# Another division of an output projection between attention's end and the loop of norm and router

## The chip, the cores and the metric

One core of a Trainium2 chip runs the whole block. The metric is device time in microseconds (us), the median of several executions. The engines are PE (TensorE, matrix products), DVE (VectorE), ACT (ScalarE), POOL (GpSimd) and SP (SyncE, which here only issues transfers). Each works through its own instructions in the order in which they stand; they wait for each other by semaphores.

## The reference

One bidirectional encoder layer on 1024 tokens of width 1024, in float32. The part around the change is this:

```python
a_out = diff_attention(q, k, v, lam, subln_g[l], lambda_init)      # 4 heads of 128 channels
p_out = multiscale_pool(u, w_pool[l], pool_scale[l])               # the mixer: 4 groups of 128
mix = jnp.concatenate([a_out, p_out], axis=-1) @ w_out[l]
x = x + g1[:, None] * mix
h = rms_norm(x, norm2_g[l]) * (1.0 + sc2[:, None]) + sh2[:, None]
y = hierarchical_moe(h, w_router_group[l], b_router_group[l], w_router_expert[l],
                     b_router_expert[l], w_gate[l], w_up[l], w_down[l])
x = x + g2[:, None] * y
```

The router picks for each token the best of 4 groups and the best two of the 8 experts in it. Each of the 32 experts then works on its tokens: `silu(x @ w_gate) * (x @ w_up) @ w_down`.

## The kernel before, in words

Tokens are worked on in 8 tiles `t` of 128 rows. A float32 product is made of three fast ones (`mm3`): each operand is split into a high and a low part, and high x high, high x low and low x high are added in PSUM.

The output projection adds up 8 blocks of 128 channels: blocks 0 to 3 are the attention heads, blocks 4 to 7 the mixer. `PARTS = [[4, 5, 6, 7], [0], [1], [2], [3]]` names five parts of it: part 0 is the mixer (4 blocks, 24 products of 128x512 for a tile), parts 1 to 4 are heads 0 to 3 (6 products each). `out_part(t, i)` makes part `i` of tile `t` on PE into a PSUM tile `pm` and adds it to the residual tile `X2[t]` on DVE: the mixer by a plain addition, a head by a scaled one, since each head has a factor by row (`Y8`) from its own norm. The pool of the `pm` tiles has two buffers.

The stages in question, in the order of the program:

- **The fill.** `attend(n)` is one step of a software pipeline through the 32 pairs of head and row tile. Its last steps, `n` from 33 to 40, have little left to do. `FILL` names them, and behind each stands the mixer part of one tile. What the projection reads is loaded by `loads`, one or two transfers behind each step (`LOADS`), in the order of that list.
- **Heads 0 and 1.** Parts 1 and 2 of all tiles follow in two rounds (`SECOND = 3`), with two loads of expert weights (`w_next`) behind each tile of the second (`EARLY1`).
- **The loop of norm and router**, `t` from 0 to 8. Round `t` makes parts 3 and 4 of tile `t`. It transposes tile `t - 1` (`flip`, PE into PSUM tiles `ph`, copied by ACT to `h2T`). It stores `X2[t]` and takes the sum of its squares (`norm2`). Then it finishes the norm of tile `t - 1` (`norm2_out`: DVE scales, POOL adds the shift `shB`, POOL's queue stores `xnd`; the last tile's shift is added by DVE) and makes its router logits (`router`, PE into `plg`).
- **Routing in batches** of tiles (`BATCH`): `route(c)` is cut into three pieces, all on DVE but for two exponentials on ACT. `rank(c)` counts on PE (`pR`) and DVE (`pk`), `place(c)` writes the tokens into the experts' lists by products on PE (`lists`). `PLAN` says behind which round each piece stands: `r` a piece of `route`, `k` `rank`, `p` `place`, `w` idle products that keep PE at work.
- **The expert loop.** POOL gathers the first tiles by the lists; then per expert 72 products of 128x512 and 12 transposes, over 12 weight tiles of 512 KB that ACT and DVE split into high and low.

SBUF has 50 slabs of 128x1024 float32. SP's loads wait in their queue until the slab that they are to fill has been read for the last time. `EARLY` says how many loads of expert weights are issued behind each round of the loop.

Where a row of the profile says L82, the helper at line 82 issued the instruction; tiles tell them apart.

Of the kernel before, what the change touches and what calls it, by code (L numbers as in the profile page):

```python
# [14 lines left out]
OP = mybir.AluOpType  # L15
# [6 lines left out]
T = S // P  # L22
KD = D // P
NH = 4
# [17 lines left out]
LOADS = {n: 1 for n in range(20, 30)}  # L42
FILL = range(33, 41)
LOAD_RATE = 2
SECOND = 3
EARLY1 = {(2, t): 2 for t in range(8)}
BATCH = [0, 0, 1, 1, 1, 2, 2, 2]
PLAN = {2: "r0", 3: "r0 r0", 4: "k0", 5: "p0 r1 r1", 6: "r1", 7: "k1", 8: "p1 w10 r2 r2 r2 k2 w4 p2"}
EARLY = {**{t: 2 for t in range(8)}, 8: 8}
ROWS = [5, 8, 11, 13]  # L50
MODS = {0: 1, 1: 2, 2: 2, **{m: 3 for m in range(3, 12)}}
WO = 7
# [16 lines left out]
def block_kernel(ctx: ExitStack, tc: tile.TileContext, A):  # L69
# [134 lines left out]
    def w_next():  # L204
        g = len(RW)
        if g < len(seq):
            e, i = seq[g]
            RW[e, i] = slab(f"we{e}_{i}")
            dma(RW[e, i], A["w_exp"][e, i])

    with tc.tile_pool(name="ps0", bufs=2, space=PSUM) as psum, tc.tile_pool(name="ps1", bufs=2, space=PSUM) as psum1, \
# [570 lines left out]
            X2[t] = slab(f"x{t}")  # L782
            dma(X2[t], A["x"][t])

        loads = [(mixer_load, 0, i, x) for i in range(2) for x in range(2)]
        loads += [(wo_load, k, x) for k in PARTS[0] for x in range(2)] + [(x_load, t) for t in range(4)]
        loads += [(mixer_load, 1, i, x) for i in range(2) for x in range(2)] + [(x_load, t) for t in range(4, T)]
        loads += [(wo_load, k, x) for k in range(NH) for x in range(2)]

        def out_part(t, i, hs=(0, 1)):  # L790

# [12 lines left out]
                dve.scalar_tensor_tensor(x, p, Y8[:, i - 1, t:t + 1], x, op0=OP.mult, op1=OP.add)  # L804

        n = FIRST
        early = [(t, 0) for t in range(T)]
        while n < N + 9 or later:
            attend(n)
            for _ in range(LOADS.get(n, LOAD_RATE if n > max(LOADS) else 0)):  # L810
                if loads:
                    fn, *args = loads.pop(0)
                    fn(*args)
            if n in FILL:
                out_part(*early.pop(0))
            n += 1
        while loads:
            fn, *args = loads.pop(0)
            fn(*args)
        for t, i in early:  # L820
            out_part(t, i)
        for i in range(1, SECOND):
            for t in range(T):
                out_part(t, i)
                for _ in range(EARLY1.get((i, t), 0)):
                    w_next()

        RK = cst.tile([P, T, 2], F32, name="RK")
        cums = cst.tile([P, T + 1, NE], BF16, name="cums")
# [25 lines left out]
        def norm2_out(t):  # L855

            xn = XN.pop(t)
            dve.scalar_tensor_tensor(xn, X2[t], RS[:, t:t + 1], MB[0], op0=OP.mult, op1=OP.mult)
            (dve if t == T - 1 else pool).tensor_tensor(xn, xn, MB[1], op=OP.add)
            (act_dma if t == T - 1 else pool_dma)(xnd[t * P:(t + 1) * P], xn)  # L860

        RT, LG = {}, {}
# [121 lines left out]
        steps = {}  # L984
        for t in range(T + 1):
            if t < T:
                for i in range(SECOND, 4):
                    out_part(t, i)
            if t >= 1:
                flip(t - 1, 0)  # L990
                flip(t - 1, 1)
            if t < T - 1:
                out_part(t, 4)
                norm2(t)
            elif t == T - 1:
                out_part(t, 4, (0,))
                out_part(t, 4, (1,))
                norm2(t)
            if t >= 1:
                norm2_out(t - 1)  # L1000
                router(t - 1)
            for _ in range(EARLY.get(t, 0)):
                w_next()
            for x in PLAN.get(t, "").split():
                c = int(x[1:])
                if x[0] == "r":
                    if c not in steps:
                        steps[c] = route(c)
                    next(steps[c], 1)
                elif x[0] == "k":  # L1010
                    rank(c)
                elif x[0] == "w":
                    warm2(c)
                else:
                    place(c)
# [321 lines left out]
```

## Time and profile before

| | us |
|---|---|
| Median of 3 runs | 1204.95 |
| The runs | 1195.96, 1205.28, 1204.95 |
| The profiled execution | 1198.64 |
| Its span, first to last instruction | 1196.9 |

| Engine | busy us | share of the span |
|---|---|---|
| PE | 1105.3 | 92% |
| DVE | 1014.7 | 85% |
| ACT | 732.4 | 61% |
| POOL | 396.8 | 33% |

The span divides into attention and what stands ahead of it (to 412.8 us), the stages that the change touches (412.8 to 572.3), the expert loop (to about 1140) and the final norm. Busy shares over the whole span say little here, since the stages have different limits; the rows below are read stage by stage. "Granted clock" (PEclk) is the share of TensorE's full clock.

### The profile page before, as it was taken

The numbers are of one execution on the slowest core, as the hardware profiler recorded it, in microseconds if no ns is written. First come the engines' busy times: TensorE is split into PE (matmuls) and PEld (weight loads), VectorE is DVE, ScalarE is ACT, GpSimd is POOL, SyncE is SP. The second block draws the span as 40 slices with busy tenths as digits, with TensorE's granted clock in tenths as the row PEclk, the third lists the DMA queues.
The fourth block names the chain that finished last, engine by engine and source line by source line (L and its number), as shares of the span: only waits on it lengthen the run. The fifth ranks groups of instructions, "written<-read, shape, count | busy, mean of one in ns | idle before, by whom it ended". The sixth has DMA issues, their size and how long they took to land.

```text
span 1196.9 us, 15760 instructions
## 1 busy us (share of the span) xinstructions
PE 1105.3 (92%) x5319; PEld 903.4 (75%) x5319; DVE 1014.7 (85%) x1187; ACT 732.4 (61%) x937; POOL 396.8 (33%) x260
## 2 busy tenths in 40 slices
PE   6696989899999999988999999999999999999975
PEld 6485866677888887777788888888888888888742
DVE  5969898868999725899899999999999999999927
ACT  5443222248888600222788888888888888888812
POOL 3546977737888600343111011011111111101001
PEclk8698999899999999977999999999999999999988
DMA  9836499489563784566699999999999999999155
GB/s 369 314 116 241 125 397 323 174 296 278 136 188 108 299 312 161 164 243 245 197 363 380 383 380 391 392 388 387 384 386 384 388 382 384 384 387 380 46 211 220
DMA packets 102950, 349.60 MB, mean 292 GB/s; under 512 B 15986, under 2 KB 16914, under 8 KB 102866
## 3 DMA queue, kind: packets, MB, share of 16 engines
q1 hardware_dynamic: 91266, 323.08, 73.9%
q0 software_dynamic: 11456, 24.96, 5.6%
q8 instruction: 43, 0.70, 0.2%
q10 hardware_dynamic: 144, 0.52, 0.1%
q14 instruction: 41, 0.34, 0.1%
HBM read 309.95 MB, written 55.33 MB: 305 GB/s over the span
## 4 chain that ended last, share of the span: by engine, by line
issue 46%; PE 26%; DVE 16%; POOL 6%; DMA 4%; ACT 1%; SPq 0%; POOLq 0%; DVEq 0%; ACTq 0%
PE pm L82 7%; PE s L82 4%; DVE wt L82 4%; PE po L82 4%; POOL x L82 4%; PE pz_v L82 3%; POOL yd L82 2%; PE pz_u L82 2%; PE pw L82 2%; DVE rt L82 2%; DMA wt<-in_w_ada 2%; DVE fy L82 1%; PE yp L82 1%; DVE wil L82 1%; DVE xn L82 1%
## 5 line engine op out<-in xcount | busy, mean ns | idle before, releaser
L82 DVE TENSOR_TENSOR wl<-we,wh 128x1024 fp32r<-128x1024 f32 x384 | 458.4, 1222 | 39.6 <-ACT wh L82 34.4
L82 ACT ACTIVATE wh<-we 128x1024 fp32r<-128x1024 f32 x384 | 399.7, 1058 | 60.5 <-PE pg L82 29.0
L82 PE MATMUL pg<-wh,xs 128*128 128x512 f32 x1024 | 338.8, 397 | 0.0
L82 PEld LDWEIGHTS pg<-wh,xs 128*128 128x128 f32 x1024 | 192.8, 188 | 39.1 <-ACT xs L82 0.2
L82 PE MATMUL pg<-wl,xs 128*128 128x512 f32 x512 | 200.0, 391 | 0.0
L82 POOL DMA_INDIRECT yd<-y,ix x32 | 32.1, 1004 | 479.6 <-ACT y L82 466.9
L82 PE MATMUL py<-wh,hth 128*128 128x512 f32 x512 | 171.9, 397 | 1.0 <-ACT hth L82 0.7
L82 PEld LDWEIGHTS py<-wh,hth 128*128 128x128 f32 x512 | 96.1, 188 | 21.8 <-DVE hth L82 1.2
L82 PEld LDWEIGHTS pg<-wl,xs 128*128 128x128 f32 x512 | 96.7, 189 | 18.2
L82 PE MATMUL py<-wl,hth 128*128 128x512 f32 x256 | 99.9, 390 | 0.0
L82 ACT ACTIVATE e<-s,mx 128x1024 f32<-128x1024 f32 x64 | 71.6, 1119 | 42.6 <-DVE mx L82 40.3
L82 DVE SCALAR_TENSOR_TENSOR wt<-wt,cB 128x1024 f32<-128x1024 f32 x48 | 91.1, 1943 | 0.8 <-ACT cB L82 0.8
L82 PE MATMUL s<-k,sq 128*128 128x512 f32 x256 | 74.0, 412 | 10.4 <-ACT e L82 10.3
L82 DVE TENSOR_REDUCE mx<-s 128x1 f32<-128x1024 f32 x64 | 78.2, 1221 | 6.0 <-PE s L82 3.2
L82 POOL TENSOR_TENSOR e<-e,e 128x1024 f32<-128x1024 f32 x32 | 76.5, 2390 | 2.7
L82 PE MATMUL po<-wh,v 128*128 128x256 f32 x256 | 60.7, 301 | 0.0
L82 PEld LDWEIGHTS s<-k,sq 128*128 128x128 f32 x256 | 44.8, 193 | 19.6 <-ACT e L82 13.1
L82 POOL DMA_INDIRECT x<-xnd,ix x32 | 46.2, 1442 | 35.3 <-PE px L82 13.6
L82 PEld LDWEIGHTS py<-wl,hth 128*128 128x128 f32 x256 | 48.2, 188 | 9.4
L82 ACT ACTIVATE xn<-x 128x1024 f32<-128x1024 f32 x7 | 7.4, 1062 | 74.1 <-DVE x L82 68.8
L82 POOL TENSOR_SCALAR e<-e,cc 128x1024 f32<-128x1024 f32 x32 | 39.2, 1225 | 37.2 <-DVE cc L82 16.7
L82 DVE SCALAR_TENSOR_TENSOR x<-pm,Y,x 128x1024 f32<-128x1024 f32 (+1 forms) x33 | 41.2, 1249 | 7.8 <-PE pm L82 6.0
(227 smaller groups left out, 2035.8 us busy)
## 6 DMA issues: line engine op xcount, KB each, us to landing
we<-in_w_exp SPq DMA_DIRECT2D x384, 512.0 KB, 6.9
wt<-in_w_ada SPq DMA_DIRECT2D x48, 512.0 KB, 8.7
win<-in_w_in SPq DMA_DIRECT2D x16, 512.0 KB, 9.1
k<-kd SPq DMA_DIRECT2D x32, 256.0 KB, 9.4
woB<-wod SPq DMA_DIRECT2D x16, 512.0 KB, 6.0
fy<-yd SPq DMA_DIRECT2D x16, 512.0 KB, 10.1
xt<-in_xT SPq DMA_DIRECT2D x8, 512.0 KB, 7.7
wo<-in_w_out SPq DMA_DIRECT2D x8, 512.0 KB, 6.6
```

Of the source, the lines that this page charges most:

```text
L82: ins = getattr(self.eng, op)(*args, **kw)
```

## The change

The mixer part and heads 0 to 2 change places. In the fill, each step is now followed by heads 0, 1 and 2 of one tile (parts 1 to 3). The two rounds of heads 0 and 1 behind the fill are gone. Round `t` of the loop makes the mixer part of tile `t`, then, behind the transposes of tile `t - 1`, head 3 as before. `loads` follows: first the residual tiles and the weights of heads 0 to 2, last the mixer tiles. DVE adds the shift for all tiles. The batches of routing are 3, 3 and 2 tiles instead of 2, 3 and 3, and `PLAN` places their pieces up to a round later. The loads of expert weights ahead of the expert loop are 32 instead of 40, none ahead of round 4.

```diff
--- before.py
+++ after.py
@@ -42,11 +42,9 @@
 LOADS = {n: 1 for n in range(20, 30)}
 FILL = range(33, 41)
 LOAD_RATE = 2
-SECOND = 3
-EARLY1 = {(2, t): 2 for t in range(8)}
-BATCH = [0, 0, 1, 1, 1, 2, 2, 2]
-PLAN = {2: "r0", 3: "r0 r0", 4: "k0", 5: "p0 r1 r1", 6: "r1", 7: "k1", 8: "p1 w10 r2 r2 r2 k2 w4 p2"}
-EARLY = {**{t: 2 for t in range(8)}, 8: 8}
+BATCH = [0, 0, 0, 1, 1, 1, 2, 2]
+PLAN = {3: "r0", 4: "r0 r0", 5: "k0", 6: "p0 r1 r1", 7: "r1 k1", 8: "p1 w10 r2 r2 r2 k2 w4 p2"}
+EARLY = {4: 6, 5: 2, 6: 4, 7: 4, 8: 16}
 ROWS = [5, 8, 11, 13]
 MODS = {0: 1, 1: 2, 2: 2, **{m: 3 for m in range(3, 12)}}
 WO = 7
@@ -782,10 +780,10 @@
             X2[t] = slab(f"x{t}")
             dma(X2[t], A["x"][t])
 
-        loads = [(mixer_load, 0, i, x) for i in range(2) for x in range(2)]
-        loads += [(wo_load, k, x) for k in PARTS[0] for x in range(2)] + [(x_load, t) for t in range(4)]
-        loads += [(mixer_load, 1, i, x) for i in range(2) for x in range(2)] + [(x_load, t) for t in range(4, T)]
-        loads += [(wo_load, k, x) for k in range(NH) for x in range(2)]
+        loads = [(x_load, 0), (x_load, 1)] + [(wo_load, k, x) for k in range(3) for x in range(2)]
+        loads += [(x_load, t) for t in range(2, T)] + [(wo_load, 3, x) for x in range(2)]
+        loads += [(wo_load, k, x) for k in PARTS[0] for x in range(2)]
+        loads += [(mixer_load, a, i, x) for a in range(2) for i in range(2) for x in range(2)]
 
         def out_part(t, i, hs=(0, 1)):
 
@@ -804,7 +802,7 @@
                 dve.scalar_tensor_tensor(x, p, Y8[:, i - 1, t:t + 1], x, op0=OP.mult, op1=OP.add)
 
         n = FIRST
-        early = [(t, 0) for t in range(T)]
+        early = list(range(T))
         while n < N + 9 or later:
             attend(n)
             for _ in range(LOADS.get(n, LOAD_RATE if n > max(LOADS) else 0)):
@@ -812,18 +810,14 @@
                     fn, *args = loads.pop(0)
                     fn(*args)
             if n in FILL:
-                out_part(*early.pop(0))
+                t = early.pop(0)
+                for i in range(1, 4):
+                    out_part(t, i)
             n += 1
         while loads:
             fn, *args = loads.pop(0)
             fn(*args)
-        for t, i in early:
-            out_part(t, i)
-        for i in range(1, SECOND):
-            for t in range(T):
-                out_part(t, i)
-                for _ in range(EARLY1.get((i, t), 0)):
-                    w_next()
+        assert not early
 
         RK = cst.tile([P, T, 2], F32, name="RK")
         cums = cst.tile([P, T + 1, NE], BF16, name="cums")
@@ -856,7 +850,7 @@
 
             xn = XN.pop(t)
             dve.scalar_tensor_tensor(xn, X2[t], RS[:, t:t + 1], MB[0], op0=OP.mult, op1=OP.mult)
-            (dve if t == T - 1 else pool).tensor_tensor(xn, xn, MB[1], op=OP.add)
+            dve.tensor_tensor(xn, xn, MB[1], op=OP.add)
             (act_dma if t == T - 1 else pool_dma)(xnd[t * P:(t + 1) * P], xn)
 
         RT, LG = {}, {}
@@ -984,8 +978,7 @@
         steps = {}
         for t in range(T + 1):
             if t < T:
-                for i in range(SECOND, 4):
-                    out_part(t, i)
+                out_part(t, 0)
             if t >= 1:
                 flip(t - 1, 0)
                 flip(t - 1, 1)
```

Three places show what that does to the order. First DVE, at the first step of the fill. `wl` and `mxl` are attention's last low parts, `x` is a residual tile and `pm` a part of the projection (its number is the part). Before:

```order
L82 SCALAR_TENSOR_TENSOR mxl_2_2984<-po_3434,mxh_2_2983 128x256
L82 TENSOR_TENSOR x_3477<-pm_0_3562,x_3477 128x1024
L82 TENSOR_TENSOR wl_1_3527<-pw_6_1_3545,wh_1_3525 128x4x128
L82 TENSOR_TENSOR wl_0_3526<-pw_7_0_3588,wh_0_3524 128x4x128
L82 COPY ss_3516<-po_3434 128x2
L82 TENSOR_TENSOR x_3479<-pm_0_3621,x_3479 128x1024
```

Now:

```order
L80 SCALAR_TENSOR_TENSOR mxl_2_2984<-po_3434,mxh_2_2983 128x256
L80 SCALAR_TENSOR_TENSOR x_2833<-pm_1_3562,Y_251,x_2833 128x1024
L80 SCALAR_TENSOR_TENSOR x_2833<-pm_2_3570,Y_251,x_2833 128x1024
L80 SCALAR_TENSOR_TENSOR x_2833<-pm_3_3578,Y_251,x_2833 128x1024
L80 TENSOR_TENSOR wl_1_3527<-pw_6_1_3545,wh_1_3525 128x4x128
L80 TENSOR_TENSOR wl_0_3526<-pw_7_0_3586,wh_0_3524 128x4x128
L80 COPY ss_3516<-po_3434 128x2
L80 SCALAR_TENSOR_TENSOR x_2891<-pm_1_3619,Y_251,x_2891 128x1024
```

One plain addition becomes three scaled ones, and attention's next instructions stand behind three evictions instead of one.

Second PE, in the loop: `ph` are the transposes of a tile, `plg` its router product, `woB` weights of the projection, `mxh` and `mxl` the heads' high and low parts, `mu` the mixer's. Before, from one router product to the head behind the next transposes:

```order
L82 MATMUL plg<-wr,h2T_4081 128x36 x8
L82 MATMUL pm_3_4126<-woB_0_3814,mxh_2_2983 128x512
L82 MATMUL pm_3_4126<-woB_1_3816,mxh_2_2983 128x512
L82 MATMUL pm_3_4126<-woB_0_3814,mxl_2_2984 128x512
L82 MATMUL pm_3_4126<-woB_0_3814,mxh_2_2983 128x512
L82 MATMUL pm_3_4126<-woB_1_3816,mxh_2_2983 128x512
L82 MATMUL pm_3_4126<-woB_0_3814,mxl_2_2984 128x512
L82 MATMUL ph_0_4135<-ident,x_3479 128x128 x4
L82 MATMUL ph_1_4141<-ident,x_3479 128x128 x4
L82 MATMUL pm_4_4147<-woB_0_3846,mxh_2_2983 128x512
L82 MATMUL pm_4_4147<-woB_1_3848,mxh_2_2983 128x512
L82 MATMUL pm_4_4147<-woB_0_3846,mxl_2_2984 128x512
```

Now, the last two of the mixer part's 24 products up to the next router product:

```order
L80 MATMUL pm_0_4044<-woB_1_3705,mu_3774 128x512
L80 MATMUL pm_0_4044<-woB_0_3703,mu_3776 128x512
L80 MATMUL ph_0_4071<-ident,x_3296 128x128 x4
L80 MATMUL ph_1_4077<-ident,x_3296 128x128 x4
L80 MATMUL pm_4_4083<-woB_0_3520,mxh_2_2983 128x512
L80 MATMUL pm_4_4083<-woB_1_3522,mxh_2_2983 128x512
L80 MATMUL pm_4_4083<-woB_0_3520,mxl_2_2984 128x512
L80 MATMUL pm_4_4083<-woB_0_3520,mxh_2_2983 128x512
L80 MATMUL pm_4_4083<-woB_1_3522,mxh_2_2983 128x512
L80 MATMUL pm_4_4083<-woB_0_3520,mxl_2_2984 128x512
L80 MATMUL plg<-wr,h2T_4070 128x36 x8
```

Head 2 (`pm_3`) has made room for the mixer part (`pm_0`) between a router product and the next transposes.

Third DVE, from the last eviction of tile 7 on. `xn` is the normed tile, `gB` its scale, `rt` a batch of routing, `ob`, `cums` and `mv` its last piece, `pk` its ranking. Before:

```order
L82 SCALAR_TENSOR_TENSOR x_3711<-pm_4_4502,Y_251,x_3711 128x512
L82 SCALAR_TENSOR_TENSOR xn_4507,ss<-x_3711 128x1024
L82 TENSOR_SCALAR n2r_m<-ss 128x1
L82 SCALAR_TENSOR_TENSOR xn_4440<-x_3709,RS,gB 128x1024
L82 SCALAR_TENSOR_TENSOR rt_4458<-plg,RS,rbias 128x36
L82 TENSOR_TENSOR pk_4530<-pR_4531,rt_4236 128x6x32
L82 TENSOR_REDUCE RK<-pk_4530 128x6
L82 TENSOR_TENSOR pk_4530<-slots,RK 128x256 x3
L82 SCALAR_TENSOR_TENSOR xn_4507<-x_3711,RS,gB 128x1024
L82 TENSOR_TENSOR xn_4507<-xn_4507,shB 128x1024
```

Now, from the norm of tile 6 on:

```order
L80 SCALAR_TENSOR_TENSOR xn_4356<-x_3477,RS,gB 128x1024
L80 TENSOR_TENSOR xn_4356<-xn_4356,shB 128x1024
L80 SCALAR_TENSOR_TENSOR rt_4482<-plg,RS,rbias 128x36
L80 TENSOR_TENSOR rt_4186<-rt_4186 128x3x32 x2
L80 TENSOR_TENSOR ob<-rt_4186 128x96
L80 TENSOR_TENSOR cums<-cums,ob 128x32 x3
L80 COPY rt_4186<-tok_104 128x6x2
L80 TENSOR_TENSOR rt_4186<-rt_4186 128x3 x2
L80 TENSOR_TENSOR mv<-rt_4186 128x576
L80 TENSOR_TENSOR pk_4504<-pR_4505,rt_4186 128x6x32
L80 TENSOR_REDUCE RK<-pk_4504 128x6
L80 TENSOR_TENSOR pk_4504<-slots,RK 128x256 x3
```

The addition of the shift and the last piece of routing (from `rt` 128x3x32 to `mv`) now stand between the norm of tile 6 and the ranking, and so ahead of the norm of tile 7.

## Rows read from the trace of the kernel before

**Rows 1.** Busy time by stretch: us, busy us (x instructions) by engine, PEclk, DMA share, GB/s

```profile
412.80:464.10 51.30, 50.44 (x251) 42.55 (x249) 12.50 (x23) 2.69 (x7) 2.44 (x2) 1.00 0.66 248
464.10:489.80 25.70, 25.70 (x103) 17.73 (x101) 21.74 (x18) 0.00 (x0) 0.00 (x0) 1.00 0.54 196
489.80:548.70 58.90, 48.87 (x276) 42.02 (x276) 53.10 (x104) 16.29 (x32) 27.94 (x35) 0.87 0.65 224
548.70:572.30 23.60, 18.97 (x117) 17.67 (x114) 20.42 (x59) 6.23 (x9) 7.37 (x6) 0.72 0.68 247
600.00:1100.00 500.00, 500.00 (x2367) 413.53 (x2365) 466.09 (x451) 428.83 (x480) 71.19 (x57) 1.00 1.00 384
```

**Rows 2.** Waits of SP's DMA queue, 560 to 1150 us: waited for, us, times, longest

```profile
SPq L103 <- DVE wl L82: 414.4, 353, 21.5
```

**Rows 3.** Timeline of PE at the end of the fill: start us, us, what

```profile
447.63 16.63 PE L82 MATMUL pm<-woB,mu 128*128 128x512 f32 x72
464.10 0.62 PE L82 MATMUL pm<-woB,mxh 128*128 128x512 f32 x2
```

**Rows 4.** Timeline of DVE, heads 0 and 1 (idle before and its releaser in brackets)

```profile
479.43 2.68 DVE L82 SCALAR_TENSOR_TENSOR x<-pm,Y,x 128x1024 f32<-128x1024 f32 x2 [0.37 <-PE pm L82]
```

**Rows 5.** Timeline of PE, one round of the loop

```profile
495.24 1.87 PE L82 MATMUL plg<-wr,h2T 128*128 128x36 f32 x16
496.94 0.70 PE L82 MATMUL pm<-woB,mxh 128*128 128x512 f32 x2
...
498.41 1.04 PE L82 MATMUL ph<-ident,x 128*128 128x128 f32 x8
499.20 0.71 PE L82 MATMUL pm<-woB,mxh 128*128 128x512 f32 x2
...
500.67 1.87 PE L82 MATMUL plg<-wr,h2T 128*128 128x36 f32 x16
```

**Rows 6.** Timeline of PE, placing, router products, first expert product

```profile
525.27 1.11 PE L82 MATMUL lists<-mv,pk 128*128 128x96 f32 x8
...
533.93 3.63 PE L82 MATMUL plg<-wr,h2T 128*128 128x36 f32 x16 [3.81 <-ACT h2T L82]
...
551.17 3.47 PE L82 MATMUL plg<-wr,h2T 128*128 128x36 f32 x16
...
572.30 0.79 PE L82 MATMUL pg<-wh,xs 128*128 128x512 f32 x1
```

**Rows 7.** Timeline of DVE, end of the loop and tail

```profile
539.48 0.42 DVE L82 TENSOR_TENSOR rt<-rt 128x96 f32<-128x96 f32 x2
...
543.93 2.13 DVE L82 SCALAR_TENSOR_TENSOR x<-pm,Y,x 128x1024 f32<-128x1024 f32 x2
546.27 0.75 DVE L82 SCALAR_TENSOR_TENSOR x<-pm,Y,x 128x512 f32<-128x512 f32 x1 [0.21 <-PE pm L82]
...
554.71 1.23 DVE L82 TENSOR_TENSOR xn<-xn,shB 128x1024 f32<-128x1024 f32 x1
```

**Rows 8.** Timeline of POOL, one add of the shift

```profile
540.40 2.35 POOL L82 TENSOR_TENSOR xn<-xn,shB 128x1024 f32<-128x1024 f32 x1
```

**Rows 9.** Timeline of DVE, instructions beside an add on POOL and the same later

```profile
540.23 2.76 DVE L82 TENSOR_TENSOR cums<-cums,ob 128x32 bf16<-128x32 bf16 x3
...
550.63 2.84 DVE L82 TENSOR_TENSOR pk<-slots,RK 128x256 f32<-128x256 f32 x3
...
561.32 0.59 DVE L82 TENSOR_TENSOR cums<-cums,ob 128x32 bf16<-128x32 bf16 x3
...
563.62 1.09 DVE L82 TENSOR_TENSOR pk<-slots,RK 128x256 f32<-128x256 f32 x3
```

**Rows 10.** Weight loads on SP, to 575 us and after: ns min/median/max, first and last start

```profile
L103 SPq DMA_DIRECT2D we<-in_w_exp x40: 327/333/1364, 421.1 to 550.2; - x40
...
L103 SPq DMA_DIRECT2D we<-in_w_exp x344: 327/328/357, 579.9 to 1092.1; - x172
```

**Rows 11.** Busy time by stretch, behind one gap of PE

```profile
533.00:541.00 8.00, 7.07 (x31) 6.38 (x32) 7.44 (x24) 2.56 (x6) 1.93 (x4) 0.57 0.67 244
```

## The prediction

> **What bounds the kernel now.** I read the table by stage first [rows 1]. From 600 to 1100 us, in the expert loop, PE is busy all of the time at full clock; DVE has 466 of 500 us, and the transfers run at 384 GB/s. Is PE or the transfer the limit there? The DMA queue of SP answers: it stood 414 us waiting for DVE to finish with a weight buffer, 353 times [rows 2]. A queue that waits for free buffers is not the one that is late, so the expert loop goes at PE's pace and its length is fixed. What can move is its first product, at 572.30, where the tail ends [rows 1].
>
> Ahead of it lie four stretches [rows 1]: the fill (412.8 to 464.1), heads 0 and 1 (to 489.8), the loop of norm and router (to 548.7), and the tail. The reader is to see who idles in each. In the fill PE has 50.4 of 51.3 us and DVE only 12.5. In the next, both are nearly full, alternating. In the loop DVE has 53.1 of 58.9, PE 48.9 and the clock is 0.87: DVE ends the waits. So DVE idles early and is late afterwards. The change trades work between those two places.
>
> **The change, step by step.** No matrix product is added or dropped. Times are the trace's.
>
> *Fill.* The 72 products between the two starts in [rows 3] take (464.10 - 447.63) / 72 = 0.229 us each, so a mixer part of 24 takes 5.49. Eight are 43.9, which leaves 51.3 - 43.9 = 7.4 us for the end of attention. Afterwards there are 24 parts of six products. At PE's pace one takes 1.37; but with two buffers of PSUM, PE and DVE alternate as they do now for heads 0 and 1: 2.68 + 0.37 = 3.05 us per two parts [rows 4]. I take that: 24 x 1.525 = 36.6, plus 7.4, is 44.0. Bounds: 40.3 if PE sets the pace (24 x 1.37 + 7.4); 48 if an eviction of about 1.3 more stands in front of three of attention's last DVE steps. The stretch of heads 0 and 1, 25.7 us, disappears. The fill ends at 412.8 + 44.0 = 456.8 instead of 489.8.
>
> *Loop.* One undisturbed round now takes 500.67 - 495.24 = 5.43 us of PE [rows 5], in which head 2's six products have 498.41 - 496.94 = 1.47. With the mixer's 24 there (5.49, and the 0.10 that changing over costs) a round takes 5.43 - 1.47 + 5.59 = 9.55. Round 0 has no transposes and no router: 5.59 + 1.47 = 7.06. Rounds 1 to 6 take 57.3. The first placing grows from 8 passes (1.11 us, [rows 6]) to 12, so at most 1.67; I take 1.4, since a row's end overlaps the next start, and 0.2 for the ranking beside it. Round 7 to the end of head 3: 5.59 + 0.79 + 1.47 = 7.85; 0.2 more until the eviction starts. So the last eviction of x7 starts at 456.8 + 7.06 + 57.3 + 1.6 + 7.85 + 0.2 = 530.8, against 546.27 now [rows 7]: 15.5 us earlier.
>
> Can DVE follow? Its round has four passes over 128x1024: mixer added, head 3, norm, shift. The shift's price is the row at 554.71, 1.23 [rows 7]; evictions go at 2.68 for two [rows 4]. With the router's small read that is about 5.2. Routing comes on top in pieces; the largest pair of pieces is some 4.5 to 4.7 us. That makes 9.9 at worst, in rounds 4 and 6, against PE's 9.55; other rounds have some 4 us to spare, and PE does not need DVE's sum for 5.59 us into the next round, since the mixer part stands first. The mixer part hides the shift's seven adds; without that cover they cost 7 x 1.23 = 8.6.
>
> *What the shift takes off.* While POOL adds the shift (2.35 us at 540.40, [rows 8]), small DVE instructions stretch: three additions of cums take 2.76 instead of 0.59, and three comparisons for pk 2.84 instead of 1.09 [rows 9]. The loop has six such stretches of about 2 us. POOL keeps only 128x1 arithmetic there. I count the stretches as gone.
>
> *Tail.* From the last eviction of x7 to the first expert product it is now 572.30 - 546.27 = 26.0 us of a DVE chain. Added: the shift of tile 6, 1.2; the last third of routing batch 1, which moves from round 6 to round 7, behind that eviction (539.48 to 543.93, less the stretch of 2.17: 2.3) [rows 7, 9]. Removed: the stretch in pk, 1.75; and about 1.0 of the smaller last batch (one comparison 0.36, one addition 0.2, a shorter list table 0.2, the rest in small change). New wait: PE's ranking of batch 1 now stands in front of the transposes of tile 7 and waits for that last third of routing, some 5 us; then the router's product runs behind it. At half clock it takes 3.47 instead of 1.87 [rows 5, 6], and DVE would wait about 0.8 for it. Sum: 26.0 + 1.2 + 2.3 - 1.75 - 1.0 + 0.8 = 27.5. The first expert product then is at 530.8 + 27.5 = 558.3, 14.0 us earlier.
>
> *Weights.* Before, 40 weight loads went out from 421.1 to 550.2, and the queue went on at 579.9 [rows 10]. Now 32 are asked for ahead; the first six go out as the fill ends, the last twelve when round 7's mixer part has released its buffers (about 526 to 528). At 0.52 MB and 384 GB/s that is 1.4 us each, 17 us: all there by 546, ahead of 558. Loading x and head weights first, and mixer tiles last, keeps the same count of loads; the mixer's land some 30 us before round 0.
>
> On that pace the Trainium skill speaks against the change ("DMA: Bandwidth & Descriptors", Bandwidth): it puts a core's share of HBM at about 358 GB/s, the side that binds. The trace disagrees, since it held 384 over 500 us [rows 1]. By the rule the expert loop would be bound by its transfers already, and the first rival below would hold.
>
> **Sum.** The profiled execution took 1198.64 us, 1.74 more than its span. 1198.64 - 14.0 = 1184.6, a ratio of 0.988. The median of the runs shown is 6.3 us above that execution; 1204.95 x 0.988 = 1190.5. I say 1190.
>
> **Rivals.**
> 1. *Transfers are the bound.* The end then follows the stream of weights. Now 344 loads go out from 579.9 to 1092.1 [rows 10]: 1.49 each. Afterwards 352 remain; if the queue resumes with the first expert product, the last goes out at 558 + 352 x 1.49 = 1082, 10 us earlier. Time 1195. Against it: 353 waits for DVE [rows 2].
> 2. *The stretches stay.* If something other than POOL's add causes them, six times 2 us remain on a DVE that has 8.6 us more to do; rounds 4 and 6 overrun, and the tail keeps 1.75 and gains 2.2. Gain about 14 - 4 - 4 = 6; time 1199. For it: the rows show two things at one time, not a cause. Against it: DVE has the same instructions unstretched where POOL is idle [rows 9].
> 3. *The clock falls in the loop (the other side).* Place: the router's product, which waits for ACT's copies; at 533.93 PE idled 3.81 us for them [rows 6], and the next 8 us ran at 0.57 [rows 11], which loses 8 x 0.43 = 3.4. One such gap costs 7 us. Two eat the gain; with four (in rounds 3 to 7) the kernel is slower by 15: 1220. Against it: each round now has 5.59 us of mixer products between ACT's exponentials and the next transposes, so they are done by then.
>
> The Trainium skill has this as a rule too ("TensorE: Matmul & The Clock Gate", HAM oscillation): idle gaps in front of bursts send the array to half rate. By that rule the wait of 5 us in the tail should be followed by half clock, as I have counted; the trace agrees (0.57 after 3.81 us, [rows 6, 11]).
>
> **How the numbers follow.** A run here can tell 1% (12 us) from no change. Forecast 0.74, its own range a gain of 10 to 18 us from the bounds of the fill (-4, +4) and of the tail's wait (0 to 2); four fifths of it lie beyond 12. Transfers 0.08, stretches 0.10, clock 0.08 (of it 0.05 slower, the rest about even). Faster by over 1%: 0.74 x 0.82 = 0.61. Slower: 0.05, and 0.01 for what I don't see: 0.06. Within 1%: the rest, 0.33. The three runs of before lie 9 us apart, so the range is taken around both ends: 1195.96 - 18 = 1178 to the median less 3, 1202. It holds the forecast, the transfers and most of the stretches.
>
> **What would show it.** Right: the fill ends near 457 with DVE above 30 us busy in it; rounds of 9.5 us with PE busy and clock 1.00 to the end of round 7; no DVE addition of 2 us or more in the loop; the last eviction of x7 near 531; 27 us of tail with PE waiting for ob ahead of the last transposes; first pg near 558, and the expert loop as long as before. Wrong: a round above 10.5 us, PE waiting for x or h2T in the loop, waits of PE or ACT for weights after 558, or a fill above 48 us.

## The result, and the profile after

| | before | after |
|---|---|---|
| Median, us | 1202.9 (4 runs) | 1186.19 (4 runs) |
| The runs, us | 1195.96, 1205.28, 1204.95, 1200.86 | 1186.88, 1188.15, 1185.5, 1185.48 |
| Ratio of after to before, 95% interval | | 0.9873 [0.9827, 0.9919] |
| The profiled execution, its span | 1198.64, 1196.9 | 1186.88, 1185.1 |

The kernel became faster by some 1.3%; the forecast was 1190 us, a ratio of 0.988. The changed kernel was later measured once more and gave 0.9917 [0.9891, 0.9944], a median of 1190.38 (run c1 below). By the medians the two measurements put the gain at 17 and at 10 us, on either side of the 1% (12 us) that the prediction said a run can tell; the forecast gain stands between them.

The stretches of the profile after, cut at the same events as [rows 1] (columns as there). They are the fill, round 0, the rounds up to the last evictions of `X2[7]` (x7 for short), the tail up to the first expert product, and the rest up to the last expert:

```profile
411.00:454.70 43.70, 42.47 (x203) 32.41 (x202) 33.22 (x39) 2.64 (x7) 2.41 (x2) 1.00 0.40 154
454.70:461.70 7.00, 7.00 (x32) 5.46 (x31) 2.53 (x3) 0.00 (x0) 0.00 (x0) 1.00 0.93 353
461.70:528.40 66.70, 66.70 (x385) 57.69 (x384) 45.33 (x95) 16.54 (x32) 18.74 (x27) 1.00 0.61 216
528.40:556.40 28.00, 19.59 (x124) 18.37 (x123) 23.20 (x71) 6.01 (x10) 5.57 (x6) 0.76 0.91 348
574.00:1122.50 548.50, 546.38 (x2580) 451.11 (x2578) 511.47 (x493) 468.40 (x523) 73.17 (x59) 1.00 0.95 364
```

The work has changed hands as the diff says. DVE has 33.2 of 43.7 us in the fill instead of 12.5 of 51.3, and PE is now busy all of the time at full clock through the whole loop, where it had 48.9 of 58.9 us at 0.87 [rows 1]. From the first to the last transposes of the expert loop (`pht`) it takes 548.8 us, in the trace of before as well (589.2 to 1138.0). SP's queue still waits for DVE most of all (from 556 us on; [rows 2]):

```profile
SPq L101 <- DVE wl L80: 367.2, 329, 21.0
```

PE's timeline (start us, us, what) around the fill's end and one round answers [rows 3, 5]:

```profile
454.67 5.67 PE L80 MATMUL pm<-woB,mu 128*128 128x512 f32 x24
...
469.49 1.87 PE L80 MATMUL plg<-wr,h2T 128*128 128x36 f32 x16
471.19 5.74 PE L80 MATMUL pm<-woB,mu 128*128 128x512 f32 x24
476.77 1.04 PE L80 MATMUL ph<-ident,x 128*128 128x128 f32 x8
477.56 0.70 PE L80 MATMUL pm<-woB,mxh 128*128 128x512 f32 x2
...
479.03 1.87 PE L80 MATMUL plg<-wr,h2T 128*128 128x36 f32 x16
```

A round takes 479.03 - 469.49 = 9.54 us, and the fill 454.67 - 410.97 = 43.7. DVE in the loop and at the end of round 7, beside [rows 7, 9]:

```profile
505.20 0.59 DVE L80 TENSOR_TENSOR cums<-cums,ob 128x32 bf16<-128x32 bf16 x3
...
512.64 1.09 DVE L80 TENSOR_TENSOR pk<-slots,RK 128x256 f32<-128x256 f32 x3
515.20 1.23 DVE L80 TENSOR_TENSOR x<-pm,x 128x1024 f32<-128x1024 f32 x1 [1.46 <-PE pm L80]
...
527.64 1.46 DVE L80 SCALAR_TENSOR_TENSOR x<-pm,Y,x 128x512 f32<-128x512 f32 x2 [0.35 <-PE pm L80]
```

The stretched additions are at their short length. DVE now waits for PE in the loop, 19.4 us in all; before, PE waited there 5.9 us for ACT's copies, which stood behind exponentials that waited for DVE, and 3.4 us for DVE itself. The tail on PE:

```profile
533.85 0.21 PE L80 MATMUL pR<-ob,tri 128*128 128x32 bf16 x1 [3.84 <-DVE ob L80]
...
535.76 1.11 PE L80 MATMUL ph<-ident,x 128*128 128x128 f32 x4 [0.37 <-DVE pk L80]
536.66 3.47 PE L80 MATMUL plg<-wr,h2T 128*128 128x36 f32 x16
...
555.08 1.07 PE L80 MATMUL px<-ident,x 128*128 128x128 f32 x8 [3.76 <-DMA x<-xnd,ix]
556.44 0.69 PE L80 MATMUL pg<-wh,xs 128*128 128x512 f32 x1 [0.30 <-ACT xs L80]
```

The first expert product starts at 556.44 instead of 572.30. Of those 15.86 us, 1.84 were there before the fill began (its first product at 410.97 against 412.81). The part that belongs to the changed stages is **14.02 us**, as forecast (14.0).

**One measure for all runs.** The first `pm` lies between 411.0 and 416.3 us in the fourteen profiles, whatever the kernel. So I compare from there, in pieces: to the norm of tile 7 (right behind its last eviction); from it to DVE's `ix`, the finished lists; from the issue of the first gather on POOL to the first `px`, the transposes of what it brought; and in all to the first `pg`. `ix` to the gather takes 0.5, `px` to `pg` 1.3 to 1.8. These are the events in before (tile 7's norm, `ix`, the gather's issue, `px`):

```profile
547.12 1.23 DVE L82 SCALAR_TENSOR_TENSOR xn<-x 128x1024 f32<-128x1024 f32 x1
...
565.72 0.22 DVE L82 TENSOR_SCALAR ix<-lists 128x64 int32<-128x64 f32 x1 [1.00 <-PE pn L82]
566.24 1.09 POOL L82 DMA_INDIRECT x<-xnd,ix  x1 [12.83 <-DVE most L82]
570.66 1.80 PE L82 MATMUL px<-ident,x 128*128 128x128 f32 x8 [2.86 <-DMA x<-xnd,ix]
```

and in after (`px` and `pg` stand above):

```profile
529.13 1.22 DVE L80 SCALAR_TENSOR_TENSOR xn<-x 128x1024 f32<-128x1024 f32 x1
...
549.24 0.23 DVE L80 TENSOR_SCALAR ix<-lists 128x64 int32<-128x64 f32 x1 [0.89 <-PE pn L80]
549.76 1.10 POOL L80 DMA_INDIRECT x<-xnd,ix  x1 [15.88 <-DVE most L80]
```

| kernel | pm to norm 7 | to ix | gather to px | pm to pg | median us | ratio to before [95%] |
|---|---|---|---|---|---|---|
| before | 134.31 | 18.60 | 4.42 | 159.49 | | |
| after | 118.16 | 20.11 | 5.32 | 145.47 | 1186.19 | 0.9873 [0.9827, 0.9919] |
| c1 (after again) | 118.20 | 20.11 | 5.15 | 145.35 | 1190.38 | 0.9917 [0.9891, 0.9944] |
| e1 shift alone | 131.05 | 18.69 | 4.51 | 156.54 | 1197.54 | 0.9981 [0.9960, 1.0001] |
| e2 shift back | 119.27 | 21.11 | 6.27 | 148.99 | 1190.31 | 0.9915 [0.9886, 0.9945] |
| e3 batches back | 117.63 | 18.67 | 5.64 | 144.28 | 1185.80 | 0.9882 [0.9845, 0.9919] |
| e4 third early | 120.24 | 17.41 | 7.49 | 147.48 | 1190.25 | 0.9921 [0.9896, 0.9946] |
| e5 ranking after | 118.16 | 19.22 | 5.49 | 144.70 | 1186.20 | 0.9890 [0.9842, 0.9938] |
| e6 loads late | 118.14 | 19.65 | 7.65 | 147.78 | 1189.41 | 0.9909 [0.9873, 0.9944] |
| e7 loads 33 on wait | 118.16 | 19.64 | 5.74 | 145.50 | 1187.06 | 0.9891 [0.9855, 0.9927] |
| e8 ranking inside | 118.43 | 16.83 | 7.80 | 145.40 | 1186.79 | 0.9892 [0.9853, 0.9931] |
| e9 loads 27 on wait | 118.14 | 19.63 | 4.44 | 144.10 | 1187.48 | 0.9916 [0.9891, 0.9940] |
| e10 both | 118.38 | 16.76 | 4.50 | 141.51 | 1181.76 | 0.9858 [0.9829, 0.9888] |
| e11 both, no wait | 118.42 | 16.81 | 4.49 | 141.66 | 1184.29 | 0.9880 [0.9858, 0.9903] |

Up to norm 7 the pieces repeat to 0.2 us where the code is the same (after, c1, e5, e7 and e9). From there to `ix` they repeat to 0.5 only: after and c1 take 20.11, e6, e7 and e9 with the same instructions in the same order 19.63 to 19.65. Their 20 idle products (`pwarm`) took 3.46 to 3.69 us instead of 4.22, and DVE did not wait 0.39 us for the ranking behind them. So a difference of half a microsecond in that piece says nothing by itself. The medians tell less, since runs of one kernel lie up to 10 us apart. The readings below go by the pieces.

### The profile page after: what moved, and what is told of

It reads as the page before. It is cut to its first block, busy times and chain, and to the rows that moved or that the text cites. A ratio compares the mean times of both kernels' runs of the same rounds, so it can differ in the third digit from the quotient of the medians.

```text
span 1185.1 us, 15743 instructions
## 1 busy us (share of the span) xinstructions
PE 1099.4 (93%) x5319; PEld 897.4 (76%) x5319; DVE 1010.2 (85%) x1194; ACT 732.7 (62%) x937; POOL 386.2 (33%) x253
## 4 chain that ended last, share of the span: by engine, by line
issue 46%; PE 29%; DVE 14%; POOL 6%; DMA 2%; ACT 1%; SPq 0%; POOLq 0%; DVEq 0%; ACTq 0%
PE pm L80 7%; DVE wt L80 4%; PE s L80 4%; PE po L80 4%; POOL x L80 4%; PE pz_v L80 3%; POOL yd L80 2%; PE pz_u L80 2%; PE pw L80 2%; DVE fy L80 1%; PE plg L80 1%; PE yp L80 1%; DVE wil L80 1%; DVE wo L80 1%; DVE mx L80 1%
## 5 line engine op out<-in xcount | busy, mean ns | idle before, releaser
L80 PEld LDWEIGHTS s<-k,sq 128*128 128x128 f32 x256 | 44.3, 191 | 18.9 <-ACT e L80 12.5
L80 PEld LDWEIGHTS py<-wl,hth 128*128 128x128 f32 x256 | 48.9, 191 | 9.7
L80 ACT ACTIVATE wh<-pw 128x512 fp32r<-128x512 f32 x64 | 38.2, 599 | 14.4 <-PE pw L80 13.7
```

The source lines that it names most:

```text
L80: ins = getattr(self.eng, op)(*args, **kw)
```

## The experiments

### The shift: e1 and e2

e1 is the kernel before with the shift moved to DVE and nothing else; e2 is the changed kernel with it moved back.

```diff
 # e1, in the kernel before
-            (dve if t == T - 1 else pool).tensor_tensor(xn, xn, MB[1], op=OP.add)
+            dve.tensor_tensor(xn, xn, MB[1], op=OP.add)
 # e2, in the changed kernel
-            dve.tensor_tensor(xn, xn, MB[1], op=OP.add)
+            (dve if t == T - 1 else pool).tensor_tensor(xn, xn, MB[1], op=OP.add)
```

> The kernel before with one line changed: the shift of tiles 0 to 6 is added by DVE instead of POOL; order, batches and loads as before. My theory (POOL's add is what stretches DVE's small instructions): no DVE instruction group of cums or pk in the loop above 1.3 us, six stretches of about 2 us gone (12 us), seven shifts of 1.23 us added (8.6 us), on a DVE that sets the loop's pace there: from the start of the fill to the first pg 1 to 5 us shorter than before's 159.5, time 0.996 to 0.999 of before. Rival (the stretches have another cause): cums and pk still take over 2.5 us, the loop gets the 8.6 us on top, first pg 7 to 9 us later, ratio 1.006 to 1.008. Second rival (the shift alone is the gain of the change): ratio 0.988.

> The changed kernel with the shift of tiles 0 to 6 back on POOL. My theory: the six stretches of about 2 us come back on DVE's small instructions in the loop (groups of cums or pk above 2.5 us), but the loop stays at PE's 9.5 us a round, because the mixer products leave DVE 1 to 3 us to spare there; the tail loses 1.2 of shift and gains a stretch of about 2: first pg 0 to 3 us later than in the changed kernel, ratio to before 0.987 to 0.990. Rival (the stretches had another cause): none comes back and DVE is 8.6 us less busy in the loop, first pg 1.2 us earlier. Second rival (the shift carried the gain): ratio 0.995 or more.

DVE in e1, the additions that were stretched in [rows 9] and a shift:

```profile
540.56 1.23 DVE L82 TENSOR_TENSOR xn<-xn,shB 128x1024 f32<-128x1024 f32 x1
542.61 0.59 DVE L82 TENSOR_TENSOR cums<-cums,ob 128x32 bf16<-128x32 bf16 x3
```

All six stretches are gone. Up to norm 7 it is 3.3 us shorter (131.05 against 134.31): five stretches leave that piece (10.6 us in all), six adds of 1.23 us come in (7.4), on an engine that set the pace. In e2 five stretches are back; two of POOL's seven adds fall into time in which DVE idles. DVE and POOL there:

```profile
503.67 0.27 DVE L80 TENSOR_REDUCE rt<-rt 128x3 f32<-128x24 f32 x2
503.89 2.15 DVE L80 TENSOR_TENSOR rt<-rt 128x24 f32<-128x24 f32 x1
...
514.00 3.30 DVE L80 TENSOR_TENSOR pk<-slots,RK 128x256 f32<-128x256 f32 x3
...
535.28 2.31 DVE L80 TENSOR_TENSOR ob<-rt 128x96 bf16<-128x96 f32 x1
```

```profile
503.61 2.39 POOL L80 TENSOR_TENSOR xn<-xn,shB 128x1024 f32<-128x1024 f32 x1
...
514.09 2.58 POOL L80 TENSOR_TENSOR xn<-xn,shB 128x1024 f32<-128x1024 f32 x1
...
535.15 2.33 POOL L80 TENSOR_TENSOR xn<-xn,shB 128x1024 f32<-128x1024 f32 x1
```

Three comparisons, of which the first starts 0.09 us before POOL's add, take 3.30 instead of 1.09; one addition that starts 0.13 behind it takes 2.31 instead of 0.26 and ends 0.11 behind POOL. So POOL's add is the cause, in both directions, and the rival of other causes falls. The Trainium skill says it so ("SBUF — State Buffer", Who interferes with whom): a DVE instruction with two inputs in SBUF and a POOL instruction that reads SBUF exclude each other, and the loser waits until the other ends. Every stretched instruction here has two SBUF inputs, and the trace agrees. It shows the other side too: two reductions with one SBUF input start at 503.67, 0.06 us behind POOL's add, and take 0.27 us together; the addition behind them, with two, takes 2.15 and ends with POOL's.

What it cost in e2 was more than expected: 3.5 us against 0 to 3. Norm 7 comes 1.1 later, the tail's chain takes 1.0 more, the gather 0.95 and `px` 0.46 more.

### The batches: e3

```diff
-BATCH = [0, 0, 0, 1, 1, 1, 2, 2]
-PLAN = {3: "r0", 4: "r0 r0", 5: "k0", 6: "p0 r1 r1", 7: "r1 k1", 8: "p1 w10 r2 r2 r2 k2 w4 p2"}
+BATCH = [0, 0, 1, 1, 1, 2, 2, 2]
+PLAN = {2: "r0", 3: "r0 r0", 4: "k0", 5: "p0 r1 r1", 6: "r1", 7: "k1", 8: "p1 w10 r2 r2 r2 k2 w4 p2"}
```

> The changed kernel with the batches 2, 3, 3 and the table of routing steps of before. My theory: batch 1 is routed in full by round 6 again, so the tail loses 2.3 us of routing, PE's wait of 3.8 us for ob and DVE's wait of 0.5 for plg, and gains about 1.0 for a last batch of three: last eviction of x7 to first pg 26 instead of 28.0, first pg about 2 us earlier than in the changed kernel, ratio to before 0.985 to 0.987. Rival (the new batches carry part of the gain): tail 29 or more, first pg 1 us or more later, ratio 0.989 or more.

From `pm` to `pg` it is 1.2 us shorter than the changed kernel: the new batches are a small loss. The expected 2 us were 1.4 in the chain up to `ix` (1.0 against e6, e7 and e9) and 0.5 in the loop; the gather took 0.3 back and the half clock of `px` 0.5.

e1 and e3 split the change: before to e1 (the shift) -2.95, e1 to e3 (division and loads) -12.26, e3 to after (batches) +1.19, in all -14.02 us. The shares hold for this order; taken out last, the shift is worth 3.5 (e2). No run has the new division without the new loads.

### The tail: e4 and e5

e4 moves the last third of batch 1's routing up a round. e5 moves the ranking of batch 1 behind tile 7's transposes and router product.

```diff
 # e4
-PLAN = {3: "r0", 4: "r0 r0", 5: "k0", 6: "p0 r1 r1", 7: "r1 k1", 8: "p1 w10 r2 r2 r2 k2 w4 p2"}
+PLAN = {3: "r0", 4: "r0 r0", 5: "k0", 6: "p0 r1 r1 r1", 7: "k1", 8: "p1 w10 r2 r2 r2 k2 w4 p2"}
 # e5
+PLAN = {3: "r0", 4: "r0 r0", 5: "k0", 6: "p0 r1 r1", 7: "r1", 8: "k1 p1 w10 r2 r2 r2 k2 w4 p2"}
```

> The changed kernel with the last third of routing batch 1 moved from round 7 to round 6, ahead of the evictions of x7. My theory: those 2.3 us fall into time in which DVE waits for PE, or push x7's evictions by at most 1; PE no longer waits 3.8 us for ob, the clock stays up for the last transposes and the router product (1.9 instead of 3.47 us): first pg 2 to 3 us earlier than in the changed kernel, tail 25 to 26 instead of 28.0, ratio to before 0.985. Rival (DVE is full in rounds 6 and 7): the last eviction of x7 comes 2.3 us later and the first pg is where it was.

> The changed kernel with the ranking of batch 1 moved behind the transposes and the router product of tile 7 (same instructions). My theory: the ranking's place is what makes PE wait (3.84 us for ob, then the second half of the transposes for the PSUM buffer that the ranking holds until DVE has read it); without that the two halves of the transposes run back to back right after x7's eviction, the router product takes 1.87 instead of 3.47 us, DVE no longer waits 0.50 us for it, and the last eviction of x7 to DVE's ix takes 20.2 to 20.5 us instead of 20.9. First pm to first pg 0.5 to 1 us shorter than the 145.5 of the changed kernel, since DVE's chain and not PE sets the tail. Rival (PE's wait of 3.84 us is on the path): 3 us shorter or more.

e4 did the opposite of what I expected: 2.0 us longer. PE in e4:

```profile
531.28 0.73 PE L80 MATMUL pm<-woB,mxh 128*128 128x512 f32 x2 [1.80 <-DVE x L80]
...
537.43 1.12 PE L80 MATMUL ph<-ident,x 128*128 128x128 f32 x4 [2.05 <-DVE pk L80]
538.34 3.47 PE L80 MATMUL plg<-wr,h2T 128*128 128x36 f32 x16
```

DVE is full in rounds 6 and 7: the third pushes x7's evictions back by 2.1, and PE waits 1.80 for a `pm` buffer. The wait for `ob` is gone, but it only hid another. Ranking and transposes share a pool of two PSUM buffers; the second half of the transposes waits until DVE has read the ranking. That wait, 0.37 us in the changed kernel, grows to 2.05, and the router product runs at half clock as before. The chain up to `ix` did become 2.7 us shorter, 0.6 more than the evictions lost; the gather took 2.2 back and the half clock of `px` 0.5.

In e5 both waits go, as PE shows:

```profile
530.46 1.07 PE L80 MATMUL ph<-ident,x 128*128 128x128 f32 x8
533.93 2.08 PE L80 MATMUL plg<-wr,h2T 128*128 128x36 f32 x16 [2.40 <-DVE rt L80]
```

The transposes run in one piece, the router product takes 2.08 instead of 3.47 us; what PE waits for now (2.40 us) is DVE's reading of the router product before it. The gain is 0.8 us (expected 0.5 to 1), and in the chain up to `ix` it is 0.9 against after but only 0.4 against e6, e7 and e9. So PE's wait of 3.84 us lay beside DVE's chain and cost almost nothing. The rival (3 us) falls.

### The weights: e6

```diff
-EARLY = {4: 6, 5: 2, 6: 4, 7: 4, 8: 16}
+EARLY = {8: 32}
```

> The changed kernel with all 32 early weight loads asked for in round 8 instead of 16 of them in rounds 4 to 7. Theory (PE sets the expert loop; transfers have room): the stream starts some 70 us later, yet first pht to last pht stays at 548.5 us. New theory on the tail (weight loads beside it stretch the gather of the first expert's rows): from the issue of the first gather to the first px 6 to 9 us instead of 5.3, and 4.4 where no loads run, as in before; total 1 to 4 us slower than the changed kernel. Rival (transfers are the bound, 1.49 us for each of 384 loads from 528): last load not before 1100 and the time 15 us or more above the changed kernel's.

```profile
L101 SPq DMA_DIRECT2D we<-in_w_exp x384: 327/328/1197, 510.4 to 1093.7; - x192
```

The stream starts at 510.4 instead of 451.8, and the last load goes out at 1093.7 instead of 1076.9; counted from the first `pm`, that is 55 us later at its start and 14 at its end. At the first `pg` 27 loads have gone out instead of 36. First to last `pht` takes 548.8 us, as always, and `pm` to `pg` is 2.3 us longer, as much as the gather grew: it takes 7.65 us instead of 5.32. Transfers have room; the first rival of the prediction falls.

### The gather: e7 and e9

Why does the gather take 4.4 to 4.5 us in before and e1, and 5.2 to 7.7 in after, c1 and e2 to e6? Both experiments put one small transfer on SP's queue, which reads the first gather's tile; the loads behind it wait until that gather has landed. In e7 that is load 33 on; in e9 only 26 are asked for ahead.

```diff
 # e7 and e9
         pool_dma(*stores.pop())
+        dma(fenced, XG[0][0:1, 0:64])
 # e9 alone
-EARLY = {4: 6, 5: 2, 6: 4, 7: 4, 8: 16}
+EARLY = {4: 6, 5: 2, 6: 4, 7: 4, 8: 10}
```

> The changed kernel with one small transfer added on the queue of the weights, ahead of load 33: it reads the first gather's rows, so that the loads from 33 on wait until that gather has landed (they started at 551.2 beside it). New theory: from the issue of the first gather to the first px 4.4 to 4.7 us, as in before, instead of 5.3 to 7.5; first pm to first pg 144 to 145; the expert loop keeps its 548.5 us, since 32 loads are there and a load takes 1.4 us like its use. Rival (the gather is slower for another reason): 5.3 us or more again. Second rival (transfers are near the bound): loop 3 us longer or more.

> The changed kernel with 26 instead of 32 weight loads asked for ahead, and the small transfer that reads the first gather's rows ahead of load 27, so that loads 27 on wait for that gather. Theory, mended (holding back only load 33 on did nothing, since loads 27 to 32, issued from 542 on, were still landing at 550): with nothing left in flight the first gather takes 4.4 to 4.7 us from its issue to the first px, as in before, instead of 5.3 to 7.8; first pm to first pg 144 to 144.6 instead of 145.5, and the expert loop keeps 548.5 us. Rival (the gather's length has nothing to do with the loads): 5.3 us or more again. Second rival (26 loads ahead are too few): waits of DVE and ACT for weights after the first pg of more than 3 us, loop longer.

e7 failed: 5.74 us. The loads from 33 on did wait (until 555.87), but that was not the whole traffic. After, SP's queue and then the transfers' share (second last column) around the gather's issue at 549.76:

```profile
507.31 37.98 SPq L101 DMA_DIRECT2D we<-in_w_exp  x20
545.69 0.38 SPq L101 DMA_DIRECT2D mvd<-mv  x1
```

```profile
546.00:549.00 3.00, 2.81 (x26) 2.61 (x25) 1.89 (x5) 0.43 (x1) 0.00 (x0) 0.94 1.02 392
549.00:552.00 3.00, 2.32 (x21) 2.13 (x20) 2.69 (x8) 0.00 (x0) 1.94 (x2) 1.00 1.00 348
```

The last of the 32 loads go out by 545.3, but the queues are full of them past the gather's issue. In e9, in the last whole stretch before its gather (issued at 553.07), the share is nothing:

```profile
549.00:552.00 3.00, 2.52 (x25) 2.32 (x24) 2.49 (x11) 1.22 (x2) 0.00 (x0) 1.00 0.00 0
```

and the gather takes 4.44 us, as in before, where the share at its issue was 0.00 too:

```profile
564.00:567.00 3.00, 2.90 (x26) 2.90 (x27) 1.93 (x10) 1.28 (x2) 0.76 (x1) 1.00 0.00 0
```

So loads of weights in flight are what lengthens it. The Trainium skill fits ("DMA: Bandwidth & Descriptors", Queues, rings and completion order): each DMA engine takes its queues in turn, so a gather shares with whatever stands in the others. The runs show the longer gather, not the turns themselves. The expert loop of e9 keeps 548.8 us with 26 loads ahead.

### A better version: e8, e10 and e11

e8 is e3 with the ranking of batch 1 between the two halves of tile 7's mixer part, where DVE waits for PE. e10 adds 24 loads ahead and the hold; e11 has the 24 loads without the hold.

```diff
 # e8, on top of e3
-PLAN = {2: "r0", 3: "r0 r0", 4: "k0", 5: "p0 r1 r1", 6: "r1", 7: "k1", 8: "p1 w10 r2 r2 r2 k2 w4 p2"}
+PLAN = {2: "r0", 3: "r0 r0", 4: "k0", 5: "p0 r1 r1", 6: "r1", 8: "p1 w10 r2 r2 r2 k2 w4 p2"}
-            if t < T:
-                out_part(t, 0)
+            if t == T - 1:
+                out_part(t, 0, (0,))
+                rank(1)
+                out_part(t, 0, (1,))
+            elif t < T:
+                out_part(t, 0)
 # e10 and e11, on top of e8; e10 has the hold of e7 besides
-EARLY = {4: 6, 5: 2, 6: 4, 7: 4, 8: 16}
+EARLY = {4: 6, 5: 2, 6: 4, 7: 4, 8: 8}
```

> The changed kernel with the batches 2, 3, 3 of before (as in the run with the batches put back), and the ranking of batch 1 issued between the two halves of tile 7's mixer part instead of behind its last head. Theory (DVE's chain sets the tail): the 1.8 us of ranking on DVE move into a wait of DVE for PE in round 7, DVE's wait of 0.5 us for the last router product goes, and the last eviction of x7 to DVE's ix takes 17 to 17.5 us instead of 19.4; first pm to first pg 142 instead of 144.3. Rival (DVE is full in round 7 too): x7's last eviction 1.8 us later, nothing gained.

> The kernel with batches 2, 3, 3 and the ranking inside tile 7's mixer part, whose shorter tail was eaten by a gather of 7.8 us; now with 24 loads ahead and loads 25 on held until the first gather has landed. Theory (the tail then ends by DVE's chain and no longer by the landing of weights): gather issue to first px 4.4 to 4.7 us, last eviction of x7 to first pg 24 to 25 us instead of 28, first pm to first pg 142 instead of 145.4; ratio to before 0.983 to 0.987. Rival (the gather is slow for another reason, or the transfers left over delay the experts): 145 again.

> The same with 24 loads ahead but nothing that holds back the rest. Theory: the queue then goes on as buffers come free, the same loads are in flight when the gather comes, and it takes 7 to 8 us again, first pm to first pg 145. Rival (the number asked for ahead decides): 4.4 to 4.7 us as with the hold.

In e8 the chain up to `ix` lost the 1.8 us (16.83 against 18.67), and norm 7 came 0.8 later than in e3. But the total is that of the changed kernel and 1.1 above e3's: the gather took 7.80 instead of 5.64. PE of e8:

```profile
558.56 1.94 PE L80 MATMUL px<-ident,x 128*128 128x128 f32 x8 [6.23 <-DMA x<-xnd,ix]
```

and of e10:

```profile
554.96 1.42 PE L80 MATMUL px<-ident,x 128*128 128x128 f32 x8 [2.93 <-DMA x<-xnd,ix]
```

With the loads out of the way it takes 4.50 us and the whole 141.5: 18.0 less than before and 4.0 less than the changed kernel. Its median (1181.76 us) is the lowest of those run, but its interval overlaps that of the changed kernel. e11 contradicts my expectation and fits its rival: without the hold the gather takes 4.49 too. SP's queue went on at 553.29 only, 1.3 us behind the gather's issue. What I had not seen is that SP reads a count (`nri`) in between, which DVE makes right behind `ix`; SP waited 7.0 us for it, and the loads not asked for ahead stand behind that. So the number asked for ahead decides, and the hold is not needed.

### The changed kernel again: c1

> The changed kernel once more, unaltered, to tell what belongs to it and what to one execution. Theory (the 4 us that its profile lost after the first pg are the clock of that execution): from the last pht to the first fgB 8.2 or 8.3 us, as in eight of the eleven other profiles, instead of 10.8; first pm to first pg 145 to 146, first gather to first px 5.3 to 5.8 us; ratio to before 0.987 to 0.991. Rival (the changed kernel brings the drop about): 10.8 us again.

(There were twelve other profiles, not eleven; eleven of them, not eight, had 8.2 or 8.3 us.) c1 has 9.3 us, between the theory and the rival. Its pieces up to `pg` are those of the first profile to 0.2 us. From the first `pg` to the end the first profile of after took 628.7 us and c1 626.4; e4 took 629.0, before 624.6 and the other ten 624.0 to 625.6. PE's last `pht` and ACT's wait for the last expert's products, in after and in e5:

```profile
1122.51 0.66 PE L80 MATMUL pht<-ident,hx 128*128 128x128 f32 x4 [1.79 <-DVE hx L80]
...
1132.51 1.11 ACT L80 ACTIVATE y<-py,LV 128x1024 f32<-128x1024 f32 x1 [8.71 <-PE py L80]
```

```profile
1122.24 0.66 PE L80 MATMUL pht<-ident,hx 128*128 128x128 f32 x4 [1.79 <-DVE hx L80]
...
1129.64 1.11 ACT L80 ACTIVATE y<-py,LV 128x1024 f32<-128x1024 f32 x1 [6.11 <-PE py L80]
```

The same 24 products behind the same gap of 1.79 us run at half clock for some 6 us in one (granted clock 0.51 from 1123 to 1130) and under 1 us in the other (1.00 from 1122.8 to 1129.8). e5, e7 and e9 share these stages with the changed kernel and have 8.2 or 8.3, so it is no fixed cost of the change. What decides it stays open.

## Why the prediction was right

**The fill** (forecast 44.0): 43.7. DVE and PE alternate as read from heads 0 and 1: from 432.93 to 435.98, two evictions take the 3.05 us of [rows 4].

**The loop** (round 0 7.06, a round 9.55, last eviction of x7 15.5 us earlier): 6.99 and 9.54, and norm 7 16.15 us earlier counted from the first `pm`. DVE followed: it waits for PE in every round but the sixth (`t` = 5), 1.0 to 4.4 us at a time in most. I had put the shift at 8.6 us without the cover of the mixer part. e1 has no such cover, and DVE gained 3.3 there all the same, since the stretches cost more than the adds; that I had not set against each other.

**The stretches** (six of about 2 us gone, one of 1.75 in the tail): confirmed by e1 and e2.

**The tail** (26.0 to 27.5). The chain from norm 7 to `ix` was to grow by 1.2 + 2.3 - 1.75 - 1.0 + 0.8 = 1.55; it grew by 1.51 (18.60 to 20.11). That is closer than it deserves: 0.5 of it are the longer idle products of this execution; the same code grew by 1.0 in e6, e7 and e9. Inside, PE's wait was 3.84 instead of 5 us and DVE's 0.50 instead of 0.8. I took the wait for `ob` for the reason of the late router product; the runs show a second one behind it, the PSUM buffer that the ranking holds (e4, e5), which I had not read from the pool.

**The mis-sized step: the weights.** I let the last twelve loads go out when round 7's mixer part releases its buffers, at 526 to 528, and land by 546. Six of them did go out by 528.4. The other six waited for the store of a normed tile; SP's queue waited 23.5 us for such stores between 505 and 556, 13.6 at a time,

```profile
SPq L101 <- DMA xnd<-xn: 23.5, 2, 13.6
```

so they went out at 542.4 to 545.3, and the queues stayed full past 550. The expert loop did not feel it (548.8 us). The gather did: 4.42 became 5.32, 0.9 us that no term of mine had. With it the tail, from the last eviction of x7 to the first expert product, took 28.1 us instead of the 27.5 of the sum. A norm 7 that came 16.15 us earlier instead of 15.5 made up for that, which is why 14.0 came out exactly. That exactness is luck; each of the two terms was off by some 0.6 us.

**The end.** I had the expert loop unchanged, and from `pht` to `pht` it is. The first profile took 4.1 us longer than before behind the first `pg`: 0.7 up to the first `pht`, 2.6 in the last expert (the clock, as above) and the rest in the final norm; c1 took 1.8 longer. So the profiled execution came out 11.8 us shorter and not 14.0: 14.0, and 1.8 from ahead of the fill, less 4.1. The median (1186.2 against 1190) is below the forecast because I had scaled a median of three runs, 1204.95, which a fourth brought to 1202.9, and because after's median does not lie above its profiled run as before's did.

**The rivals.** Transfers as the bound: refuted by e6, where a stream that ends 14 us later costs 2.3, as much as the gather grew. Stretches that stay: refuted by e1 and e2. A clock that falls in the loop: the granted clock was 1.00 from 411 to 528; the mixer products do stand between ACT's exponentials and the next transposes, and PE has no gap there. It does fall in the tail, behind the gap of 3.84 us, as counted.

## What to carry to other kernels

Where one stage idles DVE and the next idles PE, trade work between them by what each piece asks of either engine: here the parts that cost DVE as much as PE went to the stage in which DVE was idle, the part that costs PE most went to the loop that DVE held up, and that, with the loads that go with it, brought 12 of 14 us. When a chain of small steps ends in a transfer that everything waits for, shortening the chain can be worth nothing while prefetch still fills the queues, as in e8: stop the prefetch early enough that the queues are empty when it comes. And a wait that ends last on an engine may cover another for a buffer of a shared pool, so list what shares the pool before moving the first one.

## What the runs showed of the hardware

- An add of 128x1024 on POOL stops DVE's additions and comparisons with two SBUF inputs for up to its own 2.3 to 2.6 us; an addition of 0.26 us became 2.31 (e2). Reductions with one SBUF input beside the same add kept their length (two in 0.27 us).
- The transfers reached 423 GB/s over 3 us, in e8 while the gather waited:

```profile
549.00:552.00 3.00, 3.00 (x29) 3.00 (x29) 1.93 (x8) 0.00 (x0) 1.09 (x1) 1.00 1.04 423
```

- The same first gather took 4.4 to 4.5 us with no weight loads in flight at its issue (before, e1, e9, e10, e11) and 5.2 to 7.8 with them (the others). In e11 loads that went out 1.3 us behind its issue did not lengthen it.
- The same products behind the same gap of 1.79 us ran at half clock for under 1 to some 6 us, in different executions.
